# Two more raw weight buffers from the up stage on, and the token-block differences of a decoder layer in three operations set apart

## The chip, the cores and the metric

The kernel runs on one core of a Trainium2 chip. The metric is the time of one execution on the device in microseconds (us), taken as the median of several runs. Beside it stands one profiled execution, whose trace shows every instruction of TensorE (PE, with its weight loads as PEld), VectorE (DVE), ScalarE (ACT), GpSimd (POOL) and of the queue of SyncE (SP), which issues most of the loads.

## The reference, cut to what matters

One decoder layer on 256 tokens of width 1024, in float32: three token mixers side by side, a projection back, then a gated feed-forward part with a causal convolution of three taps.

```
z   = rmsnorm(x, ln1_g) @ w_in
mix = concat[pool_mixer, mLSTM, MoBA attention](z)
x   = x + mix @ w_out
u   = causal_dwconv(rmsnorm(x, ln2_g) @ w_up, ffn_conv)     # width 2 * 2816
x   = x + (silu(u[..., :2816]) * u[..., 2816:]) @ w_down
```

The change lies in the second half: from the last line of the norm before `w_up` to the end.

## The kernel before, in words

**Weights.** All weights are cut into 48 units of 128 x 2048 numbers (1 MB each), numbered in the order of use: units 0 to 10 for `w_in`, 11 to 14 for `w_out`, 15 to 36 for `w_up`, 37 to 47 for `w_down`. A product in float32 is made of three TensorE products of halves with fewer mantissa bits: each unit that was loaded ("raw") is split into `hi` (ACT copies raw, rounding it) and `lo` (DVE subtracts hi from raw), and PE multiplies hi by hi, hi by lo and lo by hi. So every unit passes through a load on SP, ACT, DVE and PE, in that order.

**Buffers.** The pool `wpool` has four raw buffers (`RAW_BUFS`), four `hi` and four `lo` slots (`HL_BUFS`). The load of unit u+4 is issued on SP as soon as the last part of unit u has been split (`split_lo` calls `load`). SP works its queue in order, so a load that waits holds back all behind it.

**Up stage.** Loop over the hidden channels, 256 at a time, one unit per turn (`up(i, 0)` and `up(i, 1)`, 32 matmuls). While PE computes turn i, ACT and DVE finish turn i-1 on their own queues, each in the order in which the code was written: `up_sum` adds the two halves of the product (z), `split_hi`/`split_lo` split later weights (lo), `up_last` and `up_taps` make the convolution (four DVE operations on fy), `up_gate` multiplies with the silu, `up_out_hi` and `up_out_lo` split the result for the down stage. A list `late` holds leftover pieces; one piece is done at the end of each turn.

**Down stage.** `w_down` has eleven units of 256 rows. Units 0 and 1, and the last two (9 and 10), are multiplied plainly (`down`, line 868). For the seven units 2 to 8 (`SEVEN`; I call them W1 to W7 here) a scheme of Strassen's kind is used (`down_seven`): two token blocks by two channel blocks by two row blocks need seven products of blocks in place of eight, 21 matmuls of 512 columns per unit (line 1258). It needs sums and differences of blocks on both sides.
- On the weights' side the sums are formed by the DMA engines: GpSimd's queue copies and accumulates blocks in DRAM (`far_step`, tiles `far`), early in the kernel, and SP later loads the result ("sum") like a unit of its own, 1 MB, next to the unit's own three blocks of 0.75 MB. An instruction `far_gate` on GpSimd holds the queue back until a certain weight of the up stage has been split.
- On the tokens' side `diffs` makes the differences on DVE in place in `a_sv`, four operations of 128 columns (line 1208). For W1 to W5 this is one piece of `late` in each of the up stage's last turns; for W6 and W7 (`n >= EARLY`) it happens in the down stage.
- `sums(i)` then splits what W needs: the three blocks of weights (lo, two operations of 768 columns), the differences (h, 512 columns, line 262), the sums (pl, two operations of 1024 columns, line 1294). W1's part is interleaved with the last turn of the up stage.

After W7 `combine` adds the products up on DVE, and the last two units end the program.

Of the kernel before, what the change touches and what calls it, by code (L numbers as in the profile page):

```python
# [134 lines left out]
def kernel(  # L135
# [14 lines left out]
    tpool = ctx.enter_context(tc.tile_pool(name="tpool", bufs=2))  # L150
# [4 lines left out]
    mpool = mix.enter_context(tc.tile_pool(name="mpool", bufs=1))  # L155
# [23 lines left out]
    def load(u):  # L179
        if u >= U_DOWN:  # L180
            if not later:
                return
            u, x = later.pop(0)
            if x:
                s_raw[u - U_DOWN] = wpool.tile([P, UMAX], F32, tag="raw", name=f"sum{u}", bufs=RAW_BUFS)
                nc.sync.dma_start(s_raw[u - U_DOWN][:, :2048], s_far[u - U_DOWN].rearrange("p b c -> p (b c)"))
                return
        n = 3 * 512 if u - U_DOWN in SEVEN else unit_cols(u)
        raw = wpool.tile([P, UMAX], F32, tag="raw", name=f"raw{u}", bufs=RAW_BUFS)
        raw_t[u] = raw  # L190
        src = wg if n == UMAX else w[u][:, :n]
        nc.sync.dma_start(raw[:, :n], src)

# [7 lines left out]
    def split_lo(u, part, parts):  # L201
        if u not in lo_t:
            lo_t[u] = wpool.tile([P, SLOT], F32R, tag="lo", name=f"lo{u}", bufs=HL_BUFS)
        n = unit_cols(u)
# [1 line left out]
        nc.vector.tensor_sub(lo_t[u][:, s], raw_t[u][:, s], hi_t[u][:, s].bitcast(F32))  # L206
# [916 lines left out]

    fpool = ctx.enter_context(tc.tile_pool(name="fpool", bufs=1))
    a_hi = fpool.tile([P, NPAIR, S], F32R, name="a_hi")
    a_lo = fpool.tile([P, NPAIR, S], F32R, name="a_lo")
    a_sv = fpool.tile([P, 2 * len(SEVEN), S], F32, name="a_sv")
    slot = {2 * i + k: 2 * n + k for n, i in enumerate(SEVEN) for k in range(2)}
# [17 lines left out]
    def up_sum(i):  # L1146
        ps = up_t[i]
        zl = big(f"zl{i}")[:, :2 * S].rearrange("p (j t) -> p j t", t=S)
# [1 line left out]
        z = big(f"z{i}")[:, :2 * S].rearrange("p (j t) -> p j t", t=S)  # L1150
        nc.vector.tensor_add(z, ps[:, :, :S], zl)  # L1151
# [46 lines left out]
    for x in far_steps:  # L1198
        if x:
            far_step(*x)  # L1200
        else:
            nc.gpsimd.tensor_copy(tpool.tile([P, 1], F32, tag="far_gate", name="far_gate"), hi_t[U_UP][:, 2047:2048].bitcast(F32))

    def diffs(i):
        n = 2 * SEVEN.index(i)
        v = [a_sv[:, n + k, t * P:t * P + P] for k in range(2) for t in range(2)]
        for o, x, y in ((3, 1, 3), (1, 1, 0), (0, 0, 3), (2, 2, 0)):
            nc.vector.tensor_sub(v[o], v[x], v[y])  # L1208
# [5 lines left out]
    late += [lambda i=i: diffs(i) for i in SEVEN[:EARLY]]

    for i in range(2, NPAIR):
# [28 lines left out]
        if i > 3 and late:  # L1245
            late.pop(0)()
# [49 lines left out]
    def sums(i):  # L1296
# [6 lines left out]
        nc.scalar.activation(hi_t[u][:, :768], raw[:, :768], AF.Copy)  # L1303
        yield
        nc.vector.tensor_sub(lo_t[u][:, :768], raw[:, :768], hi_t[u][:, :768].bitcast(F32))  # L1305
# [171 lines left out]
```

## Time and profile before

| | |
|---|---|
| median of 3 runs | 302.25 us (301.9 to 302.35) |
| the profiled execution's own time | 301.48 us |
| its span, first to last instruction | 299.7 us |
| mean granted TensorE clock | 0.999 |
| busy: PE, PEld, DVE, ACT, POOL | 292.2, 246.4, 263.3, 209.0, 45.3 us |
| moved by DMA | 75.39 MB, 252 GB/s in the mean |

A row of a timeline reads: start in us, duration in us, engine, line of the code, operation, tile written <- tiles read, shape; in brackets the idle time of the engine just before, and what ended it. An operation's duration can reach past the start of the next one on the same engine; the distance of two starts is what the engine's queue spends on it. A row of the waits reads: who waited, for whom, us in total, times, longest. The chain of waits is the work followed back from the last instruction to whatever released each step.

### The profile page before, as it was taken

The numbers are of one execution on the slowest core, as the hardware profiler recorded it, in microseconds if no ns is written. First come the engines' busy times: TensorE is split into PE (matmuls) and PEld (weight loads), VectorE is DVE, ScalarE is ACT, GpSimd is POOL, SyncE is SP. The second block draws the span as 40 slices with busy tenths as digits, with TensorE's granted clock in tenths as the row PEclk, the third lists the DMA queues.
The fourth block names the chain that finished last, engine by engine and source line by source line (L and its number), as shares of the span: only waits on it lengthen the run. The fifth ranks groups of instructions, "written<-read, shape, count | busy, mean of one in ns | idle before, by whom it ended". The sixth has DMA issues, their size and how long they took to land.

```text
span 299.7 us, 4576 instructions
## 1 busy us (share of the span) xinstructions
PE 292.2 (97%) x1609; PEld 246.4 (82%) x1609; DVE 263.3 (88%) x525; ACT 209.0 (70%) x395; POOL 45.3 (15%) x73
## 2 busy tenths in 40 slices
PE   8999999999999999999999999999999999998895
PEld 4899888788778788889888888888888888885584
DVE  2978999999986857779999999999999989898895
ACT  4767689679994646987877876777676379585710
POOL 1000104724100221501501510510211000000000
PEclk9999999999999999999999999999999999999999
DMA  7997874069967499599799999999997448899403
GB/s 252 414 419 309 335 289 140 2 160 322 207 259 285 154 303 228 118 332 355 226 265 362 230 296 346 228 284 327 227 225 240 132 140 310 298 372 363 164 1 140
DMA packets 16599, 75.39 MB, mean 252 GB/s; under 512 B 1844, under 2 KB 2240, under 8 KB 10688
## 3 DMA queue, kind: packets, MB, share of 16 engines
q1 hardware_dynamic: 9808, 59.24, 53.0%
q0 software_dynamic: 6048, 14.68, 24.5%
q10 hardware_dynamic: 720, 1.19, 1.1%
q8 instruction: 12, 0.20, 0.3%
q14 instruction: 11, 0.09, 0.1%
HBM read 74.04 MB, written 15.73 MB: 300 GB/s over the span
## 4 chain that ended last, share of the span: by engine, by line
PE 46%; DVE 29%; DMA 11%; ACT 10%; issue 3%; ACTq 0%; DVEq 0%
PE up L1141 17%; PE up L1144 9%; DVE lo L206 8%; PE wo L868 8%; DMA raw<-in_w 6%; DVE pl L1294 4%; DVE fy L1162 3%; ACT hi L199 3%; PE dn L868 3%; DVE a_sv L1208 3%; DMA head<-in_xt 2%; DMA sum<-far 2%; DVE z L1151 1%; DVE lo L1305 1%; PE upr L1086 1%
## 5 line engine op out<-in xcount | busy, mean ns | idle before, releaser
L206 DVE TENSOR_TENSOR lo<-raw,hi 128x1024 fp32r<-128x1024 f32 (+2 forms) x86 | 98.1, 1157 | 6.0 <-ACT hi L199 6.0
L199 ACT ACTIVATE hi<-raw 128x1024 fp32r<-128x1024 f32 (+2 forms) x86 | 83.0, 992 | 7.3 <-DMA raw<-in_w 5.7
L1141 PE MATMUL up<-h,hi 128*128 128x512 f32 x320 | 76.3, 391 | 0.0
L1141 PEld LDWEIGHTS up<-h,hi 128*128 128x128 f32 x320 | 58.9, 188 | 11.4
L1144 PEld LDWEIGHTS up<-h,lo 128*128 128x128 f32 x320 | 41.0, 191 | 1.5
L1144 PE MATMUL up<-h,lo 128*128 128x256 f32 x320 | 41.6, 283 | 0.0
L1162 DVE SCALAR_TENSOR_TENSOR fy<-z,par,fy 128x255 f32<-128x255 f32 (+1 forms) x80 | 33.2, 477 | 0.0
L1191 POOL DMA_DIRECT2D far<-far x14 | 11.8, 845 | 103.5 <-DMA far<-in_w 54.5
L1191 POOL DMA_DIRECT2D far<-in_w x28 | 23.0, 1286 | 7.1 <-DMA far<-in_w 7.1
L1158 ACT ACTIVATE fy<-z,par 128x256 f32<-128x256 f32 x40 | 18.0, 501 | 5.9 <-DVE z L1151 5.8
L1294 DVE TENSOR_TENSOR pl<-sum,ph 128x1024 fp32r<-128x1024 f32 x14 | 16.5, 1218 | 1.9 <-ACT ph L1293 1.9
L1151 DVE TENSOR_TENSOR z<-up,zl 128x512 f32<-128x512 f32 x20 | 13.8, 688 | 3.2 <-ACT zl L1149 2.9
L1293 ACT ACTIVATE ph<-sum 128x1024 fp32r<-128x1024 f32 x14 | 14.0, 1048 | 3.4 <-DMA sum<-far 2.4
L1172 ACT ACTIVATE fy<-fy 128x256 f32<-128x256 f32 x20 | 8.4, 418 | 11.1 <-DVE fy L1162 11.1
L1149 ACT ACTIVATE zl<-up 128x512 f32<-128x512 f32 x20 | 11.9, 593 | 5.4 <-PE up L1144 5.4
L1258 PE MATMUL m<-ph,h 128*128 128x512 f32 x42 | 14.1, 391 | 0.0
L868 PE MATMUL wo<-hi,mix_hi 128*128 128x512 f32 x32 | 11.1, 406 | 0.0
L1179 ACT ACTIVATE a_hi<-a_sv 128x256 fp32r<-128x256 f32 (+1 forms) x16 | 5.7, 370 | 7.5 <-DVE a_sv L1174 7.5
L868 PE MATMUL wo<-lo,mix_hi 128*128 128x512 f32 x32 | 10.6, 391 | 0.0
L868 PE MATMUL wo<-hi,mix_lo 128*128 128x512 f32 x32 | 10.6, 391 | 0.0
L1258 PE MATMUL m<-pl,h 128*128 128x512 f32 x21 | 8.4, 401 | 1.5 <-DVE pl L1294 1.5
L868 PE MATMUL dn<-lo,a_hi 128*128 128x512 f32 x28 | 9.6, 389 | 0.0
(323 smaller groups left out, 617.8 us busy)
## 6 DMA issues: line engine op xcount, KB each, us to landing
raw<-in_w SPq DMA_DIRECT2D x39, 1024.0 KB, 8.2
far<-in_w POOLq DMA_DIRECT2D x14, 512.0 KB, 12.0
sum<-far SPq DMA_DIRECT2D x7, 1024.0 KB, 6.6
raw<-in_w SPq DMA_DIRECT2D x7, 768.0 KB, 6.8
far<-in_w POOLq DMA_DIRECT2D x14, 256.0 KB, 12.9
far<-far POOLq DMA_DIRECT2D x14, 256.0 KB, 6.7
raw<-in_wg SPq DMA_DIRECT2D x2, 520.0 KB, 6.4
head<-in_xt ACTq DMA_DIRECT2D x4, 258.0 KB, 5.6
```

Of the source, the lines that this page charges most:

```text
L199: nc.scalar.activation(hi_t[u][:, s], raw_t[u][:, s], AF.Copy)
L206: nc.vector.tensor_sub(lo_t[u][:, s], raw_t[u][:, s], hi_t[u][:, s].bitcast(F32))
L868: nc.tensor.matmul(acc[t, c][:, :n], a, b[:, k, o:o + n], start=st and i == 0, stop=sp and i == 2)
L1141: nc.tensor.matmul(up_t[i][:, j], a, h_2[:, k].rearrange("p c t -> p (c t)"), start=k == 0, stop=False)
L1144: nc.tensor.matmul(up_t[i][:, j, :S], a, h_hi[:, k, :], start=False, stop=k == KT - 1)
L1151: nc.vector.tensor_add(z, ps[:, :, :S], zl)
L1158: nc.scalar.activation(y_t[i, j], up_t[i][j], AF.Copy, scale=pcol(Q_FC + i + NPAIR * j + 4 * NPAIR))
L1162: nc.vector.scalar_tensor_tensor(y[:, d:], up_t[i][j][:, :S - d], pcol(Q_FC + i + NPAIR * j + 2 * NPAIR * tap), y[:, d:], op0=ALU.mult, op ...
L1191: nc.gpsimd.dma_start(s_far[i][:, at, :], src[:, block:block + 1, :].to_broadcast([P, at.stop - at.start, 512]), **({"accum_op": ALU.add} ...
L1258: nc.tensor.matmul(dst, a[x], b[y], start=start and n == 0, stop=stop and n == 2)
L1293: nc.scalar.activation(h[:, s], src, AF.Copy)
L1294: nc.vector.tensor_sub(l[:, s], src, h[:, s].bitcast(F32))
```

## The change

1. The pools of the first half's temporaries (`tpool`, `mpool`) are closed as soon as the second norm has been computed, before the last quarter of unit 17 is split. The tiles of the second half (`a_hi`, `a_lo`, `a_sv`) are laid into this space there, and with them a new pool `upool`. It holds the temporaries of the up stage (`pair`, three buffers, for z and the sum in `combine`; `one`, four buffers, for fy), the tile `far_gate`, and two further raw buffers of 1 MB, `more_raw`. The rows of the first up product (`up_rows_out`) now go through `a_sv`.
2. Two loads fill the new buffers at once. From there on a load runs six units ahead, in place of four: `load_next(u, x)` issues the load of u+6 into the buffer which u has left (`home` remembers which).
3. `diffs` becomes three operations in place of four: the first makes two differences at once, 256 columns, with one operand repeated for both; the others have 128 columns. `diff_block` follows. Within a turn of the up stage the three stand apart: after the first half of lo, after a_lo, and at the turn's end.
4. In `sums` the three stand apart too, one of them ahead of each half of lo and one ahead of pl; the first half of pl comes ahead of h. For W1, the second half of lo is moved ahead of the gate, and `a_lo` of the turn before (`up_out_lo(m - 1)`) behind `sums`.

```diff
+MORE_RAW = 2
...
-    tpool = ctx.enter_context(tc.tile_pool(name="tpool", bufs=2))
+    first_half = ExitStack()
+    tpool = first_half.enter_context(tc.tile_pool(name="tpool", bufs=2))
...
-    mpool = mix.enter_context(tc.tile_pool(name="mpool", bufs=1))
+    mpool = first_half.enter_context(tc.tile_pool(name="mpool", bufs=1))
...
-    def load(u):
+    def load(u, at=None):
+        x = 0
         if u >= U_DOWN:
             if not later:
                 return
             u, x = later.pop(0)
...
+        n = 2048 if x else 3 * 512 if u - U_DOWN in SEVEN else unit_cols(u)
+        raw = at
+        if at is None:
+            raw = wpool.tile([P, UMAX], F32, tag="raw", name=f"{('raw', 'sum')[x]}{u}", bufs=RAW_BUFS)
+        home[u, x] = at
...
+    def load_next(u, x=0):
+        load(u + RAW_BUFS + len(more_raw), home.get((u, x)))
...
         if part == parts - 1:
-            load(u + RAW_BUFS)
+            load_next(u)
...
     split(f2, 2, 4)
+
+    first_half.close()
+    fpool = ctx.enter_context(tc.tile_pool(name="fpool", bufs=1))
...
+    upool = ctx.enter_context(tc.tile_pool(name="upool", bufs=1))
...
+    for n in range(MORE_RAW):
+        more_raw.append(upool.tile([P, 2048], F32, name=f"more_raw{n}"))
+        load(f2 + RAW_BUFS + n, more_raw[n])
     split(f2, 3, 4)
...
     def diffs(i):
         n = 2 * SEVEN.index(i)
-        v = [a_sv[:, n + k, t * P:t * P + P] for k in range(2) for t in range(2)]
-        for o, x, y in ((3, 1, 3), (1, 1, 0), (0, 0, 3), (2, 2, 0)):
-            nc.vector.tensor_sub(v[o], v[x], v[y])
+        v = a_sv[:, n:n + 2, :].rearrange("p k (t c) -> p (k t) c", c=P)
+        return [do(nc.vector.tensor_sub, v[:, 0:2], v[:, 1:2].to_broadcast([P, 2, P]), v[:, 0:4:3]),
+                do(nc.vector.tensor_sub, v[:, 3], v[:, 3], v[:, 0]),
+                do(nc.vector.tensor_sub, v[:, 2], v[:, 2], v[:, 3])]
...
+        *first, last = late.pop(0) if i > 3 and late else (None,)
+        first += [None] * (2 - len(first))
...
+        if first[0]:
+            first[0]()
         up_taps(m)
         if m > 2:
             up_out_lo(m - 1)
+        if first[1]:
+            first[1]()
         up_gate(m)
...
-        if i > 3 and late:
-            late.pop(0)()
+        if last:
+            last()
...
-        nc.scalar.activation(hi_t[u][:, :768], raw[:, :768], AF.Copy)
+        d = diffs(i) if n >= EARLY else ()
+        halves = slice(0, 768), slice(768, 1536)
+        if d:
+            d[0]()
+        nc.scalar.activation(hi_t[u][:, halves[0]], raw[:, halves[0]], AF.Copy)
+        nc.vector.tensor_sub(lo_t[u][:, halves[0]], raw[:, halves[0]], hi_t[u][:, halves[0]].bitcast(F32))
         yield
-        nc.vector.tensor_sub(lo_t[u][:, :768], raw[:, :768], hi_t[u][:, :768].bitcast(F32))
+        nc.scalar.activation(hi_t[u][:, halves[1]], raw[:, halves[1]], AF.Copy)
         yield
-        half_hl(hi_t[u], lo_t[u], raw[:, 768:1536], slice(768, 1536))
-        load(u + RAW_BUFS)
-        if n >= EARLY:
-            diffs(i)
+        if d:
+            d[1]()
+        nc.vector.tensor_sub(lo_t[u][:, halves[1]], raw[:, halves[1]], hi_t[u][:, halves[1]].bitcast(F32))
+        load_next(u)
+        yield
+        if d:
+            d[2]()
+        half_hl(p_hi[i], p_lo[i], s[:, :D], slice(0, D))
         hi_lo(*s_hl[i], a_sv[:, 2 * n:2 * n + 2, :].rearrange("p k t -> p (k t)"))
-        half_hl(p_hi[i], p_lo[i], s[:, :D], slice(0, D))
         half_hl(p_hi[i], p_lo[i], s[:, D:2048], slice(D, 2 * D))
-        load(u + RAW_BUFS)
+        load_next(u, 1)
         yield
...
-    up_out_lo(m - 1)
+    next(first)
     up_gate(m)
     up_out_hi(m)
     next(first)
+    up_out_lo(m - 1)
     up_out_lo(m)
```

DVE in one of the up stage's last turns, before (lo: low half of a weight; fy: convolution; a_sv<-a_sv: the differences):

```order
L1151 TENSOR_TENSOR z_2496<-up_2400,zl_2494 128x512
L206 TENSOR_TENSOR lo_2500<-raw_2276,hi_2437 128x1024
L1162 SCALAR_TENSOR_TENSOR fy_2502<-z_2496,par,fy_2502 128x255
L1162 SCALAR_TENSOR_TENSOR fy_2504<-z_2496,par,fy_2504 128x255
L1162 SCALAR_TENSOR_TENSOR fy_2502<-z_2496,par,fy_2502 128x254
L1162 SCALAR_TENSOR_TENSOR fy_2504<-z_2496,par,fy_2504 128x254
L1183 TENSOR_TENSOR a_lo<-a_sv,a_hi 128x128
L1174 TENSOR_TENSOR a_sv<-fy_2502,fy_2504 128x256
L206 TENSOR_TENSOR lo_2500<-raw_2276,hi_2437 128x1024
L1208 TENSOR_TENSOR a_sv<-a_sv 128x128 x4
```

and the same turn now:

```order
L1173 TENSOR_TENSOR z_2494<-up_2400,zl_2492 128x512
L216 TENSOR_TENSOR lo_2498<-raw_2162,hi_2437 128x1024
L891 TENSOR_TENSOR a_sv<-a_sv 128x256
L1184 SCALAR_TENSOR_TENSOR fy_2500<-z_2494,par,fy_2500 128x255
L1184 SCALAR_TENSOR_TENSOR fy_2502<-z_2494,par,fy_2502 128x255
L1184 SCALAR_TENSOR_TENSOR fy_2500<-z_2494,par,fy_2500 128x254
L1184 SCALAR_TENSOR_TENSOR fy_2502<-z_2494,par,fy_2502 128x254
L1205 TENSOR_TENSOR a_lo<-a_sv,a_hi 128x128
L891 TENSOR_TENSOR a_sv<-a_sv 128x128
L1196 TENSOR_TENSOR a_sv<-fy_2500,fy_2502 128x256
L216 TENSOR_TENSOR lo_2498<-raw_2162,hi_2437 128x1024
L891 TENSOR_TENSOR a_sv<-a_sv 128x128
```

The block of four differences at the turn's end has become three operations with other work between them.

DVE in the down stage at W6, before (h: the differences split; pl: low half of the sums):

```order
L1305 TENSOR_TENSOR lo_2945<-raw_2873,hi_2943 128x768
L1294 TENSOR_TENSOR lo_2945<-raw_2873,hi_2943 128x768
L1208 TENSOR_TENSOR a_sv<-a_sv 128x128 x4
L262 TENSOR_TENSOR h_101<-a_sv,h_101 128x512
L1294 TENSOR_TENSOR pl_2946<-sum_2881,ph_2944 128x1024 x2
```

and now:

```order
L891 TENSOR_TENSOR a_sv<-a_sv 128x256
L1337 TENSOR_TENSOR lo_2936<-raw_2827,hi_2934 128x768
L891 TENSOR_TENSOR a_sv<-a_sv 128x128
L1343 TENSOR_TENSOR lo_2936<-raw_2827,hi_2934 128x768
L891 TENSOR_TENSOR a_sv<-a_sv 128x128
L1323 TENSOR_TENSOR pl_2937<-sum_2835,ph_2935 128x1024
L272 TENSOR_TENSOR h_101<-a_sv,h_101 128x512
L1323 TENSOR_TENSOR pl_2937<-sum_2835,ph_2935 128x1024
```

Between the last difference and h, which needs it by way of ACT, stands now the first half of pl; at W1 to W5 the rows are these without the differences.

GpSimd's queue at the gate ahead of the accumulations in DRAM, before, each row with the semaphores that it waits for:

```order
L1191 DMA far_1472<-far_1472 128x512 [waits DMASW3_49]
L1202 COPY far_gate<-hi_1219 128x1 [waits Activation_49]
L1191 DMA far_1472<-far_1472 128x512 [waits DMASW7_49,DMASW2_49]
L1191 DMA far_1473<-in_w 128x2x512 [waits DMASW5_49,DMASW4_49]
L1191 DMA far_1474<-in_w 128x512
```

and now:

```order
L1213 DMA far_1478<-far_1478 128x512 [waits DMASW3_49]
L1224 COPY far_gate<-hi_1219 128x1 [waits DVE_49,PE_49,Activation_49]
L1213 DMA far_1478<-far_1478 128x512 [waits DMASW7_49,DMASW2_49]
L1213 DMA far_1479<-in_w 128x2x512 [waits DMASW5_49,DMASW4_49]
L1213 DMA far_1480<-in_w 128x512
```

The gate now also waits for DVE and PE, since its tile lies where the mixers' tiles lay; the value of PE's semaphore is that of the last product of `w_out`. The first load into a new buffer, on SP, waits for the same value.

More of the change, by code (lines that the diff above doesn't have):

```diff
@@ L168, in aux @@
         return psum.tile(shape, F32, tag="aux", name=name, bufs=4)
-    hi_t, lo_t, raw_t = {}, {}, {}
+    hi_t, lo_t, raw_t, home = {}, {}, {}, {}
+    more_raw = []
     def unit_cols(u):
@@ L183, in load @@
             u, x = later.pop(0)
[L184 to L191, printed above, removed]
+        n = 2048 if x else 3 * 512 if u - U_DOWN in SEVEN else unit_cols(u)
[3 more added lines that the diff above has]
+        home[u, x] = at
+        if x:
+            s_raw[u - U_DOWN] = raw
+            src = s_far[u - U_DOWN].rearrange("p b c -> p (b c)")
+        else:
+            raw_t[u] = raw
+            src = wg if n == UMAX else w[u][:, :n]
         nc.sync.dma_start(raw[:, :n], src)
+    def load_next(u, x=0):
+        load(u + RAW_BUFS + len(more_raw), home.get((u, x)))
     def split_hi(u, part, parts):
@@ L1088, in up_rows_out @@
     def up_rows_out(t):
-        up_r[t] = big(f"upc{t}")[:, :512]
+        up_r[t] = a_sv[:, 2 * t:2 * t + 2, :].rearrange("p j t -> p (j t)")
         nc.scalar.activation(up_r[t], up_t["r", t], AF.Copy)
@@ L1111, with pair, one @@
     split(f2, 2, 4)
+    first_half.close()
+    fpool = ctx.enter_context(tc.tile_pool(name="fpool", bufs=1))
+    a_hi = fpool.tile([P, NPAIR, S], F32R, name="a_hi")
+    a_lo = fpool.tile([P, NPAIR, S], F32R, name="a_lo")
+    a_sv = fpool.tile([P, 2 * len(SEVEN), S], F32, name="a_sv")
+    slot = {2 * i + k: 2 * n + k for n, i in enumerate(SEVEN) for k in range(2)}
+    upool = ctx.enter_context(tc.tile_pool(name="upool", bufs=1))
+    def pair(name):
+        return upool.tile([P, 2 * S], F32, tag="pair", name=name, bufs=3)
+    def one(name):
+        return upool.tile([P, S], F32, tag="one", name=name, bufs=4)
+    for n in range(MORE_RAW):
+        more_raw.append(upool.tile([P, 2048], F32, name=f"more_raw{n}"))
+        load(f2 + RAW_BUFS + n, more_raw[n])
     split(f2, 3, 4)
@@ L1121 @@
     mix.close()
[L1124 to L1128, printed above, removed]
     psum_u = ctx.enter_context(tc.tile_pool(name="psum_u", bufs=2, space=bass.MemoryType.PSUM))
@@ L1147, in up_sum @@
         ps = up_t[i]
[L1148 removed]
+        zl = pair(f"zl{i}").rearrange("p (j t) -> p j t", t=S)
         nc.scalar.activation(zl, ps[:, :, S:], AF.Copy)
[L1150 removed]
+        z = pair(f"z{i}").rearrange("p (j t) -> p j t", t=S)
         nc.vector.tensor_add(z, ps[:, :, :S], zl)
@@ L1156, in up_last @@
             n = 10 + 2 * i + j
-            y_t[i, j] = mid(f"fy{i}{j}") if i > 1 else a_sv[:, n, :]
+            y_t[i, j] = one(f"fy{i}{j}") if i > 1 else a_sv[:, n, :]
             nc.scalar.activation(y_t[i, j], up_t[i][j], AF.Copy, scale=pcol(Q_FC + i + NPAIR * j + 4 * NPAIR))
@@ L1269, in diff_block @@
     def diff_block(i, n):
-        n = (1, 3, 0, 2)[n]
+        n = (0, 1, 3, 2)[n]
         return [d[:, n * P:n * P + P] for d in s_hl[i]]
```

10 lines of the change are left out of this document (5 added, 5 removed).

## The prediction

> **What bounds the kernel now.** I read the page first, then the chain of waits, then the timelines of PE and DVE around the places that the chain names.
>
> ```profile
> PE 292.2 (97%) x1609; PEld 246.4 (82%) x1609; DVE 263.3 (88%) x525; ACT 209.0 (70%) x395; POOL 45.3 (15%) x73
> PE 46%; DVE 29%; DMA 11%; ACT 10%; issue 3%; ACTq 0%; DVEq 0%
> ```
>
> PE is busy nearly throughout, and yet less than half of the chain lies on it. The chain in order of time shows where it changes engine:
>
> ```profile
> 197.66 3.65 PE up L1141 x16
> 201.31 1.93 PE up L1144 x16
> 203.90 0.69 DVE z L1151
> ...
> 254.20 7.08 DMA sum<-far
> 261.38 1.07 ACT ph L1293
> ...
> 280.93 1.23 DVE pl L1294
> 282.21 2.11 PE m L1258 x8
> ```
>
> Up to 203 us it is PE, from 203.9 to 282.2 DVE (with one DMA), and then PE to the end. What PE loses there is read from where each W begins on it (its first product is m<-hi,a_hi; the last row is the work after W7):
>
> ```profile
> 247.37 0.39 PE L1258 MATMUL m<-hi,a_hi 128*128 128x512 f32 x1
> 252.13 0.39 PE L1258 MATMUL m<-hi,a_hi 128*128 128x512 f32 x1
> 271.22 0.39 PE L1258 MATMUL m<-hi,a_hi 128*128 128x512 f32 x1
> 277.91 0.39 PE L1258 MATMUL m<-hi,a_hi 128*128 128x512 f32 x1
> 284.83 0.61 PE L868 MATMUL dn<-hi,a_hi 128*128 128x512 f32 x2
> ```
>
> An undisturbed W takes 252.13 - 247.37 = 4.76 us. Seven would take 33.32; they take 284.83 - 247.37 = 37.46. **PE stands still for 4.14 us**, nearly all in W6 (6.69) and W7 (6.92). This is the most that the change can bring here: before W1 PE has no gap, and after W7 it runs from 284.83 to its end.
>
> **How late DVE is, and why.** In the five last turns with differences:
>
> ```profile
> 207.21 0.28 DVE L1183 TENSOR_TENSOR a_lo<-a_sv,a_hi 128x128 fp32r<-128x128 f32 x1
> 207.44 0.42 DVE L1174 TENSOR_TENSOR a_sv<-fy,fy 128x256 f32<-128x256 f32 x1
> 207.79 1.22 DVE L206 TENSOR_TENSOR lo<-raw,hi 128x1024 fp32r<-128x1024 f32 x1
> 208.92 1.26 DVE L1208 TENSOR_TENSOR a_sv<-a_sv 128x128 f32<-128x128 f32 x4
> 210.10 0.68 DVE L1151 TENSOR_TENSOR z<-up,zl 128x512 f32<-128x512 f32 x1
> 210.70 1.22 DVE L206 TENSOR_TENSOR lo<-raw,hi 128x1024 fp32r<-128x1024 f32 x1
> ```
>
> A turn on DVE takes 210.10 - 203.90 = 6.20 us, on PE 3.65 + 1.93 = 5.58. PE does not wait in the up stage, but DVE carries its lateness into the W's, where it has this rhythm:
>
> ```profile
> 249.48 0.95 DVE L1305 TENSOR_TENSOR lo<-raw,hi 128x768 fp32r<-128x768 f32 x1
> 258.70 0.95 DVE L1305 TENSOR_TENSOR lo<-raw,hi 128x768 fp32r<-128x768 f32 x1
> 262.48 2.36 DVE L1294 TENSOR_TENSOR pl<-sum,ph 128x1024 fp32r<-128x1024 f32 x2 [1.36 <-ACT ph L1293]
> 264.76 0.95 DVE L1305 TENSOR_TENSOR lo<-raw,hi 128x768 fp32r<-128x768 f32 x1
> 269.37 0.95 DVE L1305 TENSOR_TENSOR lo<-raw,hi 128x768 fp32r<-128x768 f32 x1
> 271.10 1.26 DVE L1208 TENSOR_TENSOR a_sv<-a_sv 128x128 f32<-128x128 f32 x4
> 273.06 0.69 DVE L262 TENSOR_TENSOR h<-a_sv,h 128x512 fp32r<-128x512 f32 x1 [0.70 <-ACT h L261]
> 274.01 2.36 DVE L1294 TENSOR_TENSOR pl<-sum,ph 128x1024 fp32r<-128x1024 f32 x2 [0.26 <-ACT ph L1293]
> 276.28 0.95 DVE L1305 TENSOR_TENSOR lo<-raw,hi 128x768 fp32r<-128x768 f32 x1
> 283.21 4.62 DVE L206 TENSOR_TENSOR lo<-raw,hi 128x1024 fp32r<-128x1024 f32 x4
> ```
>
> W2 and W3 take 258.70 - 249.48 = 9.22 together, 4.61 each, less than PE's 4.76. W4 (258.70 to 264.76) takes 6.06, since ACT's ph and behind it pl wait for the load of the sum. W6 takes 6.91 and W7 6.93: the differences (1.18), then 0.96 idle, because ACT's h waits for the last difference, DVE's h for ACT, and pl again for ACT.
>
> **The change part by part, on DVE's clock.**
>
> *Differences of W1 to W5, in the up stage.* Four cost 210.10 - 208.92 = 1.18. With 0.23 for the last (a_lo, of the same size, 207.21 to 207.44) this is 0.32 from start to start where one difference follows another. Set apart, I price 128 columns by a_lo, 0.23, and 256 by a_sv<-fy,fy (207.44 to 207.79), 0.35. Three then cost 0.35 + 0.23 + 0.23 = 0.81; 0.37 less, five times: **-1.85**. No row shows an operand repeated for two blocks. Bounds for the three: 0.60 (z: 512 columns in one operation, 210.10 to 210.70) and 1.18 (nothing gained). I take 0.81, the rows of the same sizes.
>
> The Trainium skill speaks against the setting apart: "VectorE: DVE Perf Modes", section "The DRAIN you can't avoid", has every operation followed by a flush that chaining does not change, and advises to lower the number of operations alone. Here the starts of a_lo and the gate lie 0.23 apart and those of the differences 0.32, so the trace does not agree. By the rule the time would be that of the second rival below.
>
> *W1.* Its second lo no longer waits for ACT, but now the first half of pl does:
>
> ```profile
> 243.43 0.42 DVE L1183 TENSOR_TENSOR a_lo<-fy,a_hi 128x256 fp32r<-128x256 f32 x1
> 245.40 0.96 DVE L1294 TENSOR_TENSOR lo<-raw,hi 128x768 fp32r<-128x768 f32 x1 [1.22 <-ACT hi L1293]
> 244.21 0.42 ACT L1179 ACTIVATE a_hi<-fy 128x256 fp32r<-128x256 f32 x1 [0.59 <-DVE fy L1174]
> 244.53 0.83 ACT L1293 ACTIVATE hi<-raw 128x768 fp32r<-128x768 f32 x1
> ```
>
> Before, from the end of fy (243.43) to W2's lo (249.48): 6.05, of it 1.22 idle. Now: lo 0.87 (269.37 to 271.10 for two such), then the gate, 0.42 until it is written, ready at 1.29; ACT's a_hi 0.32 (244.21 to 244.53), then ph 1.1 (261.38 to 262.48), so pl begins at 2.74; pl, h, pl 1.14 + 0.60 + 1.14 (4.61 less two lo; h as z, of the same size), two a_lo 0.33 each: 6.28. **+0.23**.
>
> *Deeper loads.* W4's sum was issued at 254.20, when W2's sum had been split. Six units ahead its turn comes when W1's has, about one W earlier, and it lands 7 us later while PE still has W2 before it. W4's wait goes: 6.06 - 4.61, **-1.45**. Behind it on SP stand only loads of later W's, each earlier too.
>
> *W6 and W7.* The differences cost 0.81 in place of 1.18, and h's wait (0.70) is covered by the first half of pl (1.14): 4.61 + 0.81 = 5.42, **-1.49 and -1.51**.
>
> Sum: -1.85 + 0.23 - 1.45 - 3.0 = **-6.1**: DVE would be through W7 at 277.1 in place of 283.21. PE without stalls begins W7 at 247.37 + 6 x 4.76 = 275.93 and needs h at its seventh product, 277.3, and pl at 278.2. DVE has h one pl (1.14) before its end, at 276.0. So DVE is early enough by 1.3 us, **PE loses its whole 4.14 us of stalls**, and 2 us of DVE's gain stay off the path. That 1.3 us is the cover: whatever DVE loses beyond it costs PE one for one.
>
> *What moves on the queues.* The gate on POOL and the two first new loads wait for the last product of w_out:
>
> ```profile
> 112.23 0.39 PE L868 MATMUL wo<-hi,mix_lo 128*128 128x512 f32 x1
> 102.84 0.50 POOL L1202 COPY far_gate<-hi 128x1 f32<-128x1 f32 x1 [24.34 <-ACT hi L199]
> 227.73 0.80 POOL L1191 DMA_DIRECT2D far<-far  x1 [6.02 <-DMA far<-far]
> 125.00:145.00 20.00, 20.00 (x116) 17.61 (x115) 16.54 (x26) 16.53 (x28) 1.59 (x3) 1.00 1.00 321
> far<-far POOLq DMA_DIRECT2D x14, 256.0 KB, 6.7
> ```
>
> So the gate opens at 112.6, 9.8 us later, and all accumulations behind it shift. The DMA engines are full there (share 1.00, 321 GB/s), so the 2.1 MB loaded early push them back by another 6.5. The last lands not at 227.73 + 6.7 = 234.4 but near 250.7. W7's sum is to be issued when W4's is split: 264.76, less 1.85 and 1.45, plus 0.23, near 261.7. Cover: 11 us; cost nothing.
>
> **Forecast.** The profiled execution's 301.48 (span 299.7) becomes 297.3. The runs' median lies 0.77 above that execution: 302.25 - 4.14 = **298.1 us**.
>
> **Rivals.**
>
> 1. *The loads don't land earlier* (the change doesn't do what it says), since the DMA engines are near their limit in the W's. W4's 1.45 stays; DVE ends W7 at 278.6, has h at 277.45, 0.15 late: **298.3**. For it: one W needs 1.8 MB in 4.76 us, 385 GB/s. Against it: W1 to W3's data are to be there before the W's begin. The time can't tell it from the forecast, only the waits can; I count it with the forecast.
> 2. *An operation costs its slot whatever stands beside it*: 0.32 twice and 0.42 for the 256 columns, 1.06. Up stage -0.6, W6 and W7 -1.25 each, with +0.23 and -1.45: -4.3 for DVE, h of W7 at 277.8, 0.5 late: **298.6**. Against it the 0.23 above.
> 3. *The three cost as much as the four*, through the repeated operand: 1.18. Nothing in the up stage, W6 and W7 4.61 + 1.18 (-2.26 together): -3.5, h at 278.6, 1.3 late: **299.4**. No row speaks against it.
> 4. *Slower: the late gate.* SP works in order; a sum whose blocks are not yet accumulated stops SP's queue, and with it the loads of all later W's. For pl at 278.2 W7's sum must land by 275.9 (pl 1.14 and ph 1.1 before) and be issued 7 us ahead, by 268.9. The accumulations would have to end there, 34.5 us later than now; beyond, PE loses one for one, and from 38.6 us (34.5 + 4.14) on the kernel is slower than before: 42 us late gives 302.25 + 3.4 = **305.6**. For it: the gate does open later, into full DMA engines. Against it: I count 16 us, and the six rounds that are left would each have to become some 6 us longer than present (227.73 - 102.84) / 6 = 20.8.
> 5. *No gain*: something that I don't see, say ACT (209 us busy) falling behind with the new order, holds W6 and W7 as before: **302.2**. Against it: ACT does hi, hi, ph, h, ph for one W, by the rows above at most 2 x 0.83 + 2 x 1.07 + 0.70 = 4.5, under 4.76.
>
> **How the numbers follow.** Forecast with rival 1: 0.74. Rival 2: 0.08. Rival 3: 0.08. Rival 4: 0.05. Rival 5: 0.05. The likeliest case gives 298.1. Its own range is 297.4 to 298.8: the runs before spread by 0.45, and the profiled execution lay 0.77 below their median. Rivals 2 and 3 lie above it, so I take 297.3 to 299.7, which leaves out rivals 4 and 5 and little more. A measurement of this kernel can tell 0.2% (0.6 us) from no change. Faster by more: 0.90 (forecast, rivals 1 to 3); within: 0.05; slower: 0.05.
>
> **What the profile after would show.** Right: W1 to W7 begin on PE 4.76 us apart, 7 x 4.76 = 33.3 in all, and the chain runs over PE from the up stage to the end; a difference of 128 columns takes 0.23 to the next start, one of 256 columns 0.35; turns with differences take 5.8 to 5.9 us on DVE; no wait of ph or pl for a sum; DVE idle once in W1, for ACT's ph, some 1.4 us; the last accumulation lands before W7's sum is issued. Wrong: a wait of PE on pl or h in W6 or W7 (rivals 2, 3: tell them by the operations' starts), a sum that SP holds back for far (rival 4), a gap of PE in the up stage or before the last two units, which I exclude since z, lo and the loads there only come earlier.

## The result, and the profile after

| | before | with the change |
|---|---|---|
| median of the runs made side by side | 302.3 us (4 runs, 301.9 to 302.5) | 297.2 us (4 runs, 297.05 to 297.65) |
| profiled execution | 301.48 us, span 299.7 | 297.2 us, span 295.5 |

The ratio is 0.9835, 95% interval 0.9818 to 0.9853: the change makes the kernel 5 us faster. The forecast was 298.1 (297.3 to 299.7), so the measured 297.2 lies 0.9 below the forecast and 0.1 below the lower end of its range.

The busy times and the chain of waits, after:

```profile
PE 290.3 (98%) x1609; PEld 246.3 (83%) x1609; DVE 260.6 (88%) x518; ACT 209.2 (71%) x395; POOL 45.1 (15%) x73
PE 92%; DMA 2%; DVE 2%; ACT 1%; ACTq 0%; issue 0%
```

Before, 46% of the chain lay on PE and 29% on DVE. Now 92% lie on PE: nothing else holds up the end. The timeline of PE after, where the first, second and last W begin, and the work behind W7:

```profile
247.42 0.39 PE L1287 MATMUL m<-hi,a_hi 128*128 128x512 f32 x1
...
252.18 0.39 PE L1287 MATMUL m<-hi,a_hi 128*128 128x512 f32 x1
...
275.98 0.39 PE L1287 MATMUL m<-hi,a_hi 128*128 128x512 f32 x1
...
280.74 0.61 PE L878 MATMUL dn<-hi,a_hi 128*128 128x512 f32 x2
```

280.74 - 247.42 = 33.32 us for seven W's, which is 7 x 4.76. All 4.14 us of stalls are gone (37.46 - 33.32), and the span has shrunk by 4.2. The timeline of DVE after, first one turn of the up stage from z to z, then W6's and W7's beginnings and W7's last rows:

```profile
203.94 0.69 DVE L1173 TENSOR_TENSOR z<-up,zl 128x512 f32<-128x512 f32 x1
204.55 1.22 DVE L216 TENSOR_TENSOR lo<-more_raw,hi 128x1024 fp32r<-128x1024 f32 x1
205.68 0.42 DVE L891 TENSOR_TENSOR a_sv<-a_sv 128x256 f32<-128x256 f32 x1
206.02 1.66 DVE L1184 SCALAR_TENSOR_TENSOR fy<-z,par,fy 128x255 f32<-128x255 f32 x4
207.59 0.28 DVE L1205 TENSOR_TENSOR a_lo<-a_sv,a_hi 128x128 fp32r<-128x128 f32 x1
207.80 0.28 DVE L891 TENSOR_TENSOR a_sv<-a_sv 128x128 f32<-128x128 f32 x1
208.00 0.41 DVE L1196 TENSOR_TENSOR a_sv<-fy,fy 128x256 f32<-128x256 f32 x1
208.33 1.22 DVE L216 TENSOR_TENSOR lo<-more_raw,hi 128x1024 fp32r<-128x1024 f32 x1
209.47 0.28 DVE L891 TENSOR_TENSOR a_sv<-a_sv 128x128 f32<-128x128 f32 x1
209.67 0.68 DVE L1173 TENSOR_TENSOR z<-up,zl 128x512 f32<-128x512 f32 x1
...
265.91 0.42 DVE L891 TENSOR_TENSOR a_sv<-a_sv 128x256 f32<-128x256 f32 x1
...
271.26 0.42 DVE L891 TENSOR_TENSOR a_sv<-a_sv 128x256 f32<-128x256 f32 x1
...
274.87 0.68 DVE L272 TENSOR_TENSOR h<-a_sv,h 128x512 fp32r<-128x512 f32 x1
275.47 1.22 DVE L1323 TENSOR_TENSOR pl<-more_raw,ph 128x1024 fp32r<-128x1024 f32 x1
276.61 3.49 DVE L216 TENSOR_TENSOR lo<-raw,hi 128x1024 fp32r<-128x1024 f32 x3
```

The three differences cost 0.34 + 0.20 + 0.20 = 0.74 us (205.68 to 206.02, 207.80 to 208.00, 209.47 to 209.67), in place of 1.18. The turn takes 5.73 in place of 6.20, W6 takes 271.26 - 265.91 = 5.35 and W7 276.61 - 271.26 = 5.35. DVE is through W7 at 276.61 (before: 283.21). It is through with h of W7 at 275.47; PE needs it at its seventh product, 275.98 + 6 x 0.227 = 277.34. So DVE is early by a cover of 1.87 us. No ph waits for a sum any more.

### The profile page after: what moved, and what is told of

It is laid out like the page before. It is cut to its first block, busy times and chain, and to the rows that moved or that the text cites. A ratio compares the mean times of both kernels' runs of the same rounds, so it can differ in the third digit from the quotient of the medians.

```text
span 295.5 us, 4571 instructions
## 1 busy us (share of the span) xinstructions
PE 290.3 (98%) x1609; PEld 246.3 (83%) x1609; DVE 260.6 (88%) x518; ACT 209.2 (71%) x395; POOL 45.1 (15%) x73
## 4 chain that ended last, share of the span: by engine, by line
PE 92%; DMA 2%; DVE 2%; ACT 1%; ACTq 0%; issue 0%
PE up L1163 25%; PE up L1166 13%; PE wo L878 8%; PE dn L878 6%; PE m L1287 6%; PE dn L1287 5%; DMA head<-in_xt 2%; PE B L490 1%; PE V L490 1%; PE V L492 1%; PE V L491 1%; PE upr L1096 1%; PE B L492 1%; PE upr L1095 1%; PE B L491 1%; PE A L490 1%
## 5 line engine op out<-in xcount | busy, mean ns | idle before, releaser
L216 DVE TENSOR_TENSOR lo<-raw,hi 128x1024 fp32r<-128x1024 f32 (+2 forms) x74 | 83.5, 1148 | 6.7 <-ACT hi L209 6.7
L209 ACT ACTIVATE hi<-raw 128x1024 fp32r<-128x1024 f32 (+2 forms) x74 | 70.3, 983 | 7.6 <-DMA raw<-in_w 6.0
L216 DVE TENSOR_TENSOR lo<-more_raw,hi 128x1024 fp32r<-128x1024 f32 x12 | 14.6, 1215 | 0.0
L209 ACT ACTIVATE hi<-more_raw 128x1024 fp32r<-128x1024 f32 x12 | 12.6, 1052 | 0.0
L1322 ACT ACTIVATE ph<-sum 128x1024 fp32r<-128x1024 f32 x8 | 8.4, 1055 | 3.1 <-PE dn L1287 2.3
L1323 DVE TENSOR_TENSOR pl<-sum,ph 128x1024 fp32r<-128x1024 f32 x8 | 9.7, 1216 | 0.0
```

The source lines that it names most:

```text
L209: nc.scalar.activation(hi_t[u][:, s], raw_t[u][:, s], AF.Copy)
L1323: nc.vector.tensor_sub(l[:, s], src, h[:, s].bitcast(F32))
```

## The experiments

Each was run beside the kernel before on the same chip; ratios are against that kernel. Three of them (the kinds of differences and the two more profiles of the kernel before) are a single execution each. Gains are given from the medians and from the spans of the profiled executions, which can be followed in the timelines. A span is one execution, and executions differ by up to nearly 3 us before the up stage; where that matters, I count from the beginning of W1 on PE. Where the difference comes from is the last experiment.

**The two buffers alone.** From the change, the differences and the order of the down stage were put back:

```diff
-        return [do(nc.vector.tensor_sub, v[:, 0:2], ...), do(...), do(...)]
+        for o, x, y in ((3, 1, 3), (1, 1, 0), (0, 0, 3), (2, 2, 0)):
+            nc.vector.tensor_sub(v[o], v[x], v[y])
...
-        half_hl(p_hi[i], p_lo[i], s[:, :D], slice(0, D))
         hi_lo(*s_hl[i], a_sv[:, 2 * n:2 * n + 2, :].rearrange("p k t -> p (k t)"))
+        half_hl(p_hi[i], p_lo[i], s[:, :D], slice(0, D))
```

> The two more buffers alone, with the four differences in a block and the old order of the down stage. Theory (DVE is late, and each thing that makes it late is paid one for one until PE's 4.14 us are used up): only the wait of W4's ph for its sum goes, DVE is through W7 1.45 us earlier (283.21 becomes about 281.8), and since PE waits for DVE all that time, the whole 1.45 comes out: about 300.8 us. W6 and W7 still take 6.9 us each on DVE. Rival (the loads are the whole change): about 297.2, as with the change. Rival (loads landing early are worth nothing): 302.2, with W4's turn on DVE still 6.06 us.

Measured: 300.17 us beside 301.91, ratio 0.9939 (0.9912 to 0.9967); span 298.5. The timeline of DVE, first lo of W4 and of W5, and the first row behind W7:

```profile
258.85 0.95 DVE L1333 TENSOR_TENSOR lo<-more_raw,hi 128x768 fp32r<-128x768 f32 x1
...
263.45 0.95 DVE L1333 TENSOR_TENSOR lo<-raw,hi 128x768 fp32r<-128x768 f32 x1
...
281.92 4.62 DVE L216 TENSOR_TENSOR lo<-raw,hi 128x1024 fp32r<-128x1024 f32 x4
```

W4 takes 4.60 in place of 6.06, and DVE is through at 281.92, as expected (281.8). The span is 1.2 shorter than before. W1 began on PE 0.13 later than before in this execution (247.50); from there to the work behind W7 (283.56) PE takes 36.06 us, 1.40 less than the 37.46 before, where 1.45 was expected. The earlier load is worth what the wait was, and it is not the whole change.

**Everything but the buffers.** One number of the change:

```diff
-MORE_RAW = 2
+MORE_RAW = 0
```

> The change with no additional raw buffer: the new pools, order and three differences stay. Theory: W4's wait for its sum comes back (DVE's turn of W4 about 6.0 us in place of 4.6) and is swallowed by the cover, which the profile after puts at 1.8 us (h of W7 written at 275.5, needed at 277.3): 297.2 to 297.6 us, seven W's still about 4.76 us apart on PE. Rival (a wait for a load costs its length, or more in runs without the profiler): 298.6 us or more.

Measured: 298.11 us beside 301.91, ratio 0.9865 (0.9831 to 0.9900). Timelines of DVE, where the wait is back, and of PE, W7 and what follows:

```profile
266.27 1.23 DVE L1323 TENSOR_TENSOR pl<-sum,ph 128x1024 fp32r<-128x1024 f32 x1 [0.84 <-ACT ph L1322]
...
278.28 0.39 PE L1287 MATMUL m<-hi,a_hi 128*128 128x512 f32 x1
...
283.04 0.39 PE L878 MATMUL dn<-hi,a_hi 128*128 128x512 f32 x1
```

A wait for a sum came back, at W5 this time and with 0.84 us, and PE did not feel it: all seven W's take 4.76, as W7 does here. That agrees with a cover that swallows it. The median does not confirm it as well: 298.11 lies 0.5 above the range that was expected (297.2 to 297.6), and the profiled execution, one of the slowest of its six, had lost 2.3 us in the first half (its W1 begins at 249.72). Whether the buffers are worth nothing or up to 1 us on top of the rest is not settled by these runs.

**The differences in the up stage alone.** The kernel before with the new `diffs` for W1 to W5 and the old four for W6 and W7:

```diff
+        if first[0]:
+            first[0]()
         up_taps(m)
...
         if n >= EARLY:
-            diffs(i)
+            diffs_four(i)
```

> The kernel before with the three differences set apart in the up stage's five turns only; W6 and W7 and all buffers as before. Theory: PE waits for nothing in the up stage, yet DVE carries its gain of 5 x 0.44 = 2.2 us (1.18 to 0.74 each) into the W's, where PE waits for it: about 300.1 us, PE's stalls still in W6 and W7, 2.2 us shorter together. Rival (an operation on an engine that nobody waits for at that place is worth nothing): 302.2.

Measured: 298.92 us beside 301.91, ratio 0.9888 (0.9853 to 0.9924); span 297.2, 2.5 less than before. The first row behind W7 on DVE, then on PE:

```profile
280.66 4.63 DVE L206 TENSOR_TENSOR lo<-raw,hi 128x1024 fp32r<-128x1024 f32 x4
...
282.28 0.39 PE L868 MATMUL dn<-hi,a_hi 128*128 128x512 f32 x1
```

DVE is 2.55 us earlier (283.21 to 280.66) and so is PE (284.83 to 282.28): one for one, from operations at a place where PE waits for nothing. The whole execution was 0.44 us ahead already when the up stage began (the first z on DVE at 131.15, before 131.59). So 2.1 us belong to the edit, as the 2.2 of the differences let expect. The median, 298.92, lies 1.2 below the 300.1 that was expected; its six runs spread from 297.4 to 300.4.

**The down stage's order alone.** The kernel before with the new `sums` and the new order around W1; the four differences stay in a block in the up stage:

```diff
-    late += [lambda i=i: diffs(i) for i in SEVEN[:EARLY]]
+    late += [lambda i=i: diffs_four(i) for i in SEVEN[:EARLY]]
...
-        half_hl(hi_t[u], lo_t[u], raw[:, 768:1536], slice(768, 1536))
+        if d:
+            d[1]()
+        nc.vector.tensor_sub(lo_t[u][:, halves[1]], raw[:, halves[1]], ...)
```

> The kernel before with the new order of the down stage only (W1's lo, pl ahead of h, the three differences of W6 and W7 set apart), the up stage's four differences in a block as before. Theory: DVE's turns of W6 and W7 go from 6.9 to 5.35 each, W1's grows by about 0.2: through W7 at about 280.3. In the new order PE's last wait is the one for h (one pl, 1.14, before the end, with 15 of 21 products, 3.4 us, still to run), in the old one for the first pl (1.05 before the end, 2.6 to run), so PE ends W7 at about 282.6 in place of 284.83: 2.3 us, 300.0 us. Rival (what DVE gains comes out whole): 299.3. The gains of the three single parts, 1.45 + 2.2 + 2.3 = 5.9, are then more than the 4.14 of stalls that there were.

Measured: 300.2 us beside 301.91, ratio 0.9925 (0.9896 to 0.9953); span 298.6, only 1.1 less. DVE at W5, and PE behind W7:

```profile
268.12 1.23 DVE L1301 TENSOR_TENSOR pl<-sum,ph 128x1024 fp32r<-128x1024 f32 x1 [2.12 <-ACT ph L1300]
...
283.82 0.39 PE L868 MATMUL dn<-hi,a_hi 128*128 128x512 f32 x1
```

W6 and W7 became shorter as expected, 5.35 each, but the wait for a sum moved from W4 to W5 and grew from 1.36 to 2.12 us, and took back 0.8. So a load that is issued one W ahead is not late by a fixed amount. DVE had lost another 0.4 us in the up stage, where ACT waited 0.75 us for a weight (at 204.50). So DVE was through W7 at 281.71 in place of the expected 280.3. Counted from the beginning of W1 (247.25), DVE is 1.4 us earlier than before and PE 0.9: here not all of it comes out, as was expected of the new order.

By the ratios the three single parts gain 0.6 + 1.1 + 0.75 = 2.5%, the whole change 1.65%. From the beginning of W1 to the work behind W7, PE gains 1.4 + 2.1 + 0.9 = 4.4 us by the parts and 4.14 by the whole: together the parts meet the end of PE's stalls.

**What makes a difference cheap.** The change, with the differences of W1 to W5 done in five ways, two of them followed by four superfluous ones:

```diff
+        def free():
+            s = parts()
+            nc.vector.tensor_sub(s[0], q[0], q[1])
+            nc.vector.tensor_sub(s[1], q[0], q[1])
...
+        def chained():
+            s = parts()
+            nc.vector.tensor_sub(s[0], q[0], q[1])
+            nc.vector.tensor_sub(s[1], s[0], q[1])
```

> The change, with the differences of W1 to W5 done in five ways, each operation on a line of its own where it counts: W1 four in a block at the turn's end; W2 four set apart; W3 the new three in a block; W4 three apart and then four more of 128 columns into a spare tile that read the same two blocks and need nothing of each other; W5 three apart and then four more that each need the result of the one before. Theory (an operation that needs the result of the one just ahead waits for it, another starts at once): in W4's four the starts lie 0.20 us apart, in W5's chain about 0.4; in W1's block 0.20 where the next needs nothing of the one ahead and about 0.4 where it does, 0.98 over three; set apart each costs 0.20 to 0.23, so that W2's four cost 0.8 to 0.9, little more than the new three (0.74); W3's block costs about 1.0 to 1.2. Rival (an operation costs its slot whatever stands beside it, as the Trainium skill has it in VectorE: DVE Perf Modes, The DRAIN you can't avoid): all four in a row lie equally far apart, in W4 as in W5, and W2 costs four slots, 1.2. Rival (the number of operations is what counts): W3 costs 0.74 as a block too. Time by the theory: some 2.5 to 3 us more work on DVE than with the change against a cover of 1.8, so about 1 us more than the change.

Measured, a single execution: 298.48 us, 1.3 above the change's 297.2, where about 1 was expected. The timeline of DVE: W1's block of four; then four that need nothing of each other; then four that each need the one before; z is what comes next:

```profile
209.47 0.28 DVE L1237 TENSOR_TENSOR a_sv<-a_sv 128x128 f32<-128x128 f32 x1
209.78 0.29 DVE L1239 TENSOR_TENSOR a_sv<-a_sv 128x128 f32<-128x128 f32 x1
210.11 0.29 DVE L1241 TENSOR_TENSOR a_sv<-a_sv 128x128 f32<-128x128 f32 x1
210.44 0.29 DVE L1243 TENSOR_TENSOR a_sv<-a_sv 128x128 f32<-128x128 f32 x1
210.65 0.68 DVE L1173 TENSOR_TENSOR z<-up,zl 128x512 f32<-128x512 f32 x1
...
228.46 0.29 DVE L1251 TENSOR_TENSOR scratch<-a_sv 128x128 f32<-128x128 f32 x1
228.66 0.28 DVE L1252 TENSOR_TENSOR scratch<-a_sv 128x128 f32<-128x128 f32 x1
...
235.12 0.29 DVE L1257 TENSOR_TENSOR scratch<-a_sv 128x128 f32<-128x128 f32 x1
235.44 0.29 DVE L1258 TENSOR_TENSOR scratch<-scratch,a_sv 128x128 f32<-128x128 f32 x1
235.77 0.29 DVE L1259 TENSOR_TENSOR scratch<-scratch,a_sv 128x128 f32<-128x128 f32 x1
```

The same operation of 128 columns holds DVE for 0.20 us where the next one needs nothing of it, and for 0.32 to 0.33 where it does. The rival by which an operation costs its slot whatever stands beside it falls. So does the rival by which only their number counts: the new three in a block cost 0.99, not 0.74. My own theory was too high for the chain, where it had about 0.4, and wrong at one point: I expected 0.20 from the first of the block of four to the second, since the second reads no result of the first. It is 0.31. The second overwrites what the first reads, and the program then makes it wait for DVE's own semaphore just as for a result:

```
L1237 TENSOR_TENSOR a_sv<-a_sv 128x128
L1239 TENSOR_TENSOR a_sv<-a_sv 128x128 [waits DVE_49]
...
L1251 TENSOR_TENSOR scratch<-a_sv 128x128
L1252 TENSOR_TENSOR scratch<-a_sv 128x128
```

So what costs 0.12 us is a wait of the engine for its own last operation, and any other operation in between hides it. Four set apart (W2) cost 0.20 + 0.21 + 0.21 + 0.20 = 0.82; the new three in a block (W3) cost 0.99; three apart 0.74. Of the 0.44 that the change gains per unit, 0.36 come from the distance and 0.08 from the fewer operations.

**The cover.** The change with two, then six superfluous operations of 512 columns at the beginning of W6:

```diff
+        if n == 5:
+            e = pair("extra")
+            for _ in range(6):
+                nc.vector.tensor_sub(e, h_2[:, 0]..., h_2[:, 2]...)
```

> The change, with two superfluous operations of 512 columns on DVE at the beginning of W6 (0.60 us each, 1.2 together). Theory: the cover after the change is 1.8 us (h of W7 is written at 275.5 and needed at 277.3), so DVE is through W7 1.2 us later and PE waits for nothing: the time of the change, W's on PE still 4.76 us apart. Rival (DVE still sets the end): 1.2 us more.

> The change, with six such operations at the beginning of W6 (3.6 us). Theory: 3.6 less the cover of 1.8 comes out one for one: 1.8 us more than the change, with PE waiting for h in W6 (3.6 less 2.5 there) and in W7. Rival (DVE has been taken off the path): no difference. Rival (everything comes out): 3.6 us more.

> The kernel with the change, once more, beside the kernel before in more rounds and on the same chip as the two runs with more work on DVE. Theory (the kernel before loses to the loads' varying times what the change's six buffers hide: 0.8 us on the runs' median more than in the profiled execution): the change's runs lie closer together than those of the kernel before, and the ratio of the medians stays near 0.983 to 0.986, more than the profiled 4.1 to 4.3 us (0.986). Rival (the 0.8 us was chance): ratio 0.986 and equal spreads.

Measured on one chip: the change again 297.17 us (ratio 0.9827, 0.9799 to 0.9856), with two more operations 297.04 (ratio 0.9829, 0.9798 to 0.9861), with six 299.29 (ratio 0.9916, 0.9883 to 0.9948). The change's runs lie within 0.6 us and those of the kernel before within 2.6, as the theory of the repetition had it; its reason for that, the hidden loads, is not what the last experiment shows. With six, the extra operations on DVE and two rows of PE, W7's beginning and its wait:

```profile
265.75 4.31 DVE L1336 TENSOR_TENSOR extra<-h 128x512 f32<-128x512 f32 x6
...
277.41 0.39 PE L1287 MATMUL m<-hi,a_hi 128*128 128x512 f32 x1
...
279.69 0.50 PE L1287 MATMUL dn<-hi,h 128*128 128x512 f32 x1 [0.29 <-DVE h L272]
```

Two operations vanish in the cover: the seven W's still take 33.33 us on PE. Six take 4.24 us to the next start, not 3.6, because each overwrites the one before and waits for it (5 x 0.12). Less the cover of 1.87 that leaves 2.4; PE's seven W's became 2.2 us longer, the median 2.1. (The bracket of the last row counts only 0.29 as idle; the row itself begins 2.35 us later than in the change, at 279.69 in place of 277.34.) So DVE is off the path by nearly 2 us, and beyond them it is on it again, nearly one for one.

**The gate, earlier.** The gate's tile was put into another pool, so that it waits for the split weight alone:

```diff
-upool.tile([P, 1], F32, name="far_gate")
+cpool.tile([P, 1], F32, name="far_gate")
```

> The change, with the gate's tile put where nothing was before, so that the gate waits for the split weight only and opens near 103 us, as in the kernel before, in place of 112.8. Theory: accumulations and gate have 11 us of cover or more (the last accumulation was issued at 242.2 after, the load of W7's sum at 261.4), so an earlier gate is worth nothing: the time of the change, the last accumulation some 6 to 10 us earlier. Rival (the late gate costs something through the DMA engines): 0.6 us or more faster than the change.

Measured: 299.22 us beside 301.79, ratio 0.9914 (0.9886 to 0.9942): 2 us slower than the change, which neither theory had. The last accumulation was issued at 233.07 in place of 242.15, and no W waited; but PE itself was slower. Its timeline in W1:

```profile
249.93 0.39 PE L1287 MATMUL m<-hi,a_hi 128*128 128x512 f32 x1
...
251.30 0.39 PE L1287 MATMUL dn<-hi,h 128*128 128x512 f32 x1
...
254.09 0.39 PE L1287 MATMUL dn<-ph,a_hi 128*128 128x512 f32 x1
254.31 0.39 PE L1287 MATMUL dn<-pl,a_hi 128*128 128x512 f32 x1
```

The twelve matmuls that read h, the differences, take (254.09 - 251.30) / 12 = 0.233 us each; the six before them, which read a_hi or a_lo, take 0.228, about as before. The granted clock was 1.00 here. A W takes 4.84 us, and each of the twenty turns of the up stage, where every product reads the same tile, 5.63 in place of 5.57: 0.6 and 1.2 us in all, 1.8 of the 2. What the edit did beside the gate: the small tile lies ahead of the weights' slots and of a_hi now and moved all of them by 32 bytes (a_hi from 143136 to 143168, a slot of hi from 75552 to 75584), while the tile of h stayed at 25888.

The gate itself can't be the reason for the pace. It opened at 104.44, and 60 us earlier the products A<-hi,h were slow already: 48 of them, from 31.82 to 42.79, begin 0.233 us apart, with the change (32.38 to 43.06) 0.227. Up to the gate the two programs have the same instructions in the same order and differ in the addresses alone. That makes the addresses the likely cause; no run moved them with the gate left as it was. So the experiment does not answer its question by the time. Its trace adds only that no W waited with either gate.

**The gate, much later.** The accumulations' program was moved behind the fifth turn of the up stage:

```diff
         if last:
             last()
+        if i == 4:
+            open_far(u + 3)
```

> The change, with the gate held until a weight of the fifth turn of the up stage has been split, near 138 us, some 25 us later than with the change (112.8). Theory (rival 4 of the prediction, made true): the accumulations shift by as much, the last lands near 249 + 25 = 274; SP holds the load of W7's sum until then, 13 us later than it would issue it (261.4), and 5 us later than PE can bear (268.9), so PE waits for pl of W7, or of W6 too, and the time grows by some 5 us, to about 302. Rival (accumulations that start later meet fewer other loads and catch up): the last lands before 269, and the time is that of the change.

Measured: 306.08 us beside 301.79, ratio 1.0126 (1.0096 to 1.0155). The gate on POOL, the last accumulation, the load of W7's sum on SP, ACT that waits for it, and PE:

```profile
139.58 0.32 POOL L1232 COPY far_gate<-hi 128x1 f32<-128x1 f32 x1 [61.27 <-ACT hi L209]
...
271.39 0.80 POOL L1213 DMA_DIRECT2D far<-far  x1 [4.67 <-DMA far<-far]
...
276.60 0.33 SPq L199 DMA_DIRECT2D more_raw<-far  x1
...
281.79 1.06 ACT L1325 ACTIVATE ph<-more_raw 128x1024 fp32r<-128x1024 f32 x1 [10.53 <-DMA more_raw<-far]
...
283.42 0.79 PE L1290 MATMUL dn<-hi,h 128*128 128x512 f32 x1 [6.21 <-ACT h L271]
...
290.06 0.61 PE L878 MATMUL dn<-hi,a_hi 128*128 128x512 f32 x2
```

The gate opens 26.8 us later than with the change, the last accumulation is issued 29.2 us later: nothing is caught up. SP holds W7's sum back until 276.60, and PE waits 6.21 us, near the 5 expected; the time was expected at about 302 and is 4 us longer. The other 3 us come from PE itself: after the pause the clock is low, 0.50 to 0.55 in the windows from 282 to 290 us, and the 15 products left of W7 take from 283.42 to 290.06, 6.64 us in place of 3.40 (15 x 0.227). 6.21 + 3.24 = 9.45; the span is 9.3 longer than after the change.

**Why the kernel before is spread so much.** In the three series of experiments 10 of its 32 runs took more than 302.5 us, the others 301.0 to 302.5; the change's nine runs lie within 296.7 to 297.65. Two more profiles of the kernel before:

> The kernel before, for one more profile. Runs in which DVE sets the end (before, and the change with six more operations) were spread over 2 us and more, those in which PE sets it over 0.6. Theory: the slower ones lose it in waits of DVE for loads, above all for the sums of W4 and W5, which are issued one W ahead and took 5 to 7.6 us: a slower profile shows longer such waits. Rival: DVE's operations themselves last longer, or DVE falls behind in the up stage.

> The kernel before, for a further profile, to the same question: with 0.8 us between the profiled execution and the median, one of two more profiles should lie at or above the median, and its waits against the first profile's tell where it loses.

Measured: 301.34 and 303.58 us. The view of windows (us; then busy time of PE, PEld, DVE, ACT, POOL, granted clock, DMA) from 45 to 50 us, first of the faster, then of the slower; and in the slower one the wait of PE:

```profile
45.00:50.00 5.00, 4.89 (x43) 4.43 (x42) 4.81 (x12) 4.57 (x15) 2.04 (x7) 1.00 0.46 164
```

```profile
45.00:50.00 5.00, 3.28 (x25) 2.67 (x24) 4.84 (x11) 4.97 (x12) 0.70 (x3) 0.87 0.13 31
50.00:55.00 5.00, 5.00 (x30) 4.82 (x30) 4.86 (x13) 3.98 (x9) 2.69 (x6) 0.79 0.43 179
...
48.51 1.50 PE L685 MATMUL mS<-mqT,mkT 64*128 64x256 f32 x8 [1.72 <-DVE mkT L538]
```

Both theories fall. The W's are as before in both (W1 to W7: 30.75 and 30.59 us); the two differ by 2.4 us when z of the third up unit is added (131.25 and 133.63), so here the time is lost in the first half. There a load of a weight landed late (ACT's hi waited for it until 38.26 in the one and 40.12 in the other), PE paused for 1.72 us, and then got a clock of 0.87 and 0.79. The run without the additional buffers shows the same: a pause of 1.83 us at the same product, a clock of 0.90 and 0.76, W1 at 249.72. The change touches nothing there, and it does not prevent the pause: two runs built on it, the five kinds of differences and the early gate, paused at the same product for 1.02 and 1.42 us, with the clock at 1.00. That none of the change's nine runs took as much longer is, as far as I can tell, chance. The slower profile is one further execution; that it speaks for the ten runs above 302.5 is not shown.

## Why the prediction was right

*Bound.* "PE stands still for 4.14 us", and the change brings this and no more: 4.14 in the W's, 4.2 in the span. The reading of the chain, that DVE's lateness of the up stage is paid in the W's, is shown by the up-stage experiment.

*Differences.* Priced at 0.81, they cost 0.74; the turns gain 0.44 in place of 0.37, five times. The rows of the same sizes were the right ones; the operand that is repeated for two blocks costs nothing (0.34 for 256 columns, as the gate's product: 208.00 to 208.33). Rivals 2 (1.06) and 3 (1.18) fall. The prediction set a section of the Trainium skill against this (VectorE: DVE Perf Modes, The DRAIN you can't avoid). It left out that the same section has an operation that is not held start earlier; the advice on the number of operations stands on the same page, under Rules for kernel authors. The rows here show such a difference, 0.20 without a wait and 0.32 with one.

*W1, +0.23.* The wait is there as forecast:

```profile
243.91 1.23 DVE L1323 TENSOR_TENSOR pl<-more_raw,ph 128x1024 fp32r<-128x1024 f32 x1 [1.44 <-ACT ph L1322]
```

From z to W2's lo it is 9.38 us (238.09 to 247.47), before 9.17 (240.31 to 249.48): +0.21.

*Deeper loads, -1.45.* Shown by the buffers alone. As a part of the whole they end in the cover; rival 1, which was counted with the forecast since the time could not tell them apart, did not come true in the waits.

*W6 and W7, 5.42 each.* 5.35.

*Sum.* DVE through W7 at 277.1; it was 276.61. Cover 1.3; it was 1.87, and two experiments measured it.

*Gate.* The gate opened at 112.76 (forecast 112.6). The last accumulation was issued at 242.15 and W7's sum at 261.40 (261.7). The 6.5 us by which the new loads were to push the accumulations came out as 14.4 - 9.9 = 4.5 (227.73 to 242.15, less the gate's delay from 102.84). Rival 4 counted the pause of PE but not the low clock after it. By its price a sum issued at 276.60 in place of 268.9 costs 7.7 us; the much later gate cost 6.21 of pause and 3.24 of low clock.

*The time.* 298.1 was forecast, 297.2 measured. The mechanism came out, the size of the last term did not. The step that failed is the last: "the runs' median lies 0.77 above that execution", which I carried over to the kernel after. The profiled execution after lies on its median. So the stalls account for 4.14 of the 5.1 us. On the chip where the change was run again, the medians differ by 4.66, and by 4.4 if the four runs of the kernel before above 302.5 are left out (301.57 against 297.17). What the runs of the first comparison lost beyond that, no profile shows; it stays open.

## What to carry to other kernels

An engine that nobody waits for at a place can still be what is waited for 60 us later: follow its lateness to where the chain changes engine, and price the edit there, up to the stalls that exist. Small operations that depend on each other, also by overwriting what the one ahead reads, are best placed between others; here that was worth more than having fewer of them. Adding one tile can move all that lies behind it, so compare addresses before a side effect is put down to the schedule.

## What the runs showed of the hardware that I had not expected

- A DVE operation that overwrites what its predecessor reads is as late as one that needs its result: 0.31 us from start to start in place of 0.20 at 128 columns.
- With the weights' slots moved by 32 bytes against the tile of h, the matmuls that read both began 0.233 us apart in place of 0.227, at full granted clock. Only one kernel shows it, no run moved the addresses alone, and which distances are bad was not tried.
- PE's clock falls after a pause and stays low for a while: 0.50 to 0.55 after 6.2 us, and 0.87 then 0.79 in two windows of 5 us around and after a pause of 1.72 us (0.90 and 0.76 with 1.83 us); with 1.42 us, in the run with the early gate, it stayed at 1.00. The Trainium skill, TensorE: Matmul & The Clock Gate, section Part 1: The HAM clock gate, has half the clock after an idle window of about 3.4 us. The long pause agrees with it; the drop after 1.72 us comes earlier than that.
- A 1 MB load from DRAM took 5.1 to 7.6 us from issue to the first instruction that used it, where that instruction waited for it: both ends are from one execution, that of the down stage's order alone (W3's sum, 249.52 to 254.57, and W5's, 259.41 to 267.03). A buffer that is just deep enough in one execution is not in the next.
